# Seven products for six of eight chunk pairs in the up projection, the first conv tap on ScalarE, and five raw buffers

## The chip, the core and the metric

The kernel runs on one core of a Trainium2 chip. The core has engines that run side by side, each with its own queue in program order: TensorE (PE in the profile, with its weight loads as PEld), VectorE (DVE), ScalarE (ACT), GpSimd (POOL) and SyncE (SP), which here only issues DMAs. They wait for each other by semaphores. The metric is the device time of one execution in microseconds; a run of the kernel is compared by the median of its times.

## The reference

One layer of a hybrid encoder for 256 prompt frames and 8 streams of 16 frames, together 384 frames ("tokens", three blocks of 128), all in float32. The part that matters here is the feed-forward half:

```python
h2 = rmsnorm(x, norm_ffn_g)
up = h2 @ w_up                       # (384, 2048) @ (2048, 11264)
g_half, u_half = up[..., :D_FF], up[..., D_FF:]      # D_FF = 5632
ext_f = concat([ffn_buf, g_half])
gc = causal_dwconv(ext_f, ffn_dw_w, ffn_dw_b)        # 3 taps per column
x = x + (silu(gc) * u_half) @ w_down                 # (384, 5632) @ (5632, 2048)
```

The two last gate rows per stream (`new_ffn`) are outputs too.

## The kernel before

Every float32 matrix product is done with operands split in two: `hi` is the value rounded to the type that TensorE multiplies fast, `lo` is the rest, and each product takes three matmuls (hi by hi, hi by lo, lo by hi; function `three`, lines 1352 to 1354). A weight tile of two 128-row chunks and 512 columns (512 KB) is loaded by SP into a raw buffer, copied to `hi` by ScalarE (`CAST hi<-raw`) and reduced to `lo` by VectorE (`TENSOR_TENSOR lo<-raw,hi`).

The feed-forward part works in eleven groups of 512 gate columns and the 512 up columns that belong to them. The order is: up 0, then for g = 1 to 10 up g and down g-1, then down 10. Groups 0 and 10 do the up projection plainly: 16 chunks, 2 column halves, 3 token blocks, 3 matmuls, 288 in all. Groups 1 to 9 save matmuls: for a pair of feature chunks (2k, 2k+1), with token blocks 0 and 1 and the gate and up columns, the four-by-two product is done in the Strassen-Winograd way, with seven products where eight stand in the plain form; token block 2 is done plainly. The sums of activation blocks that it needs are made once (`sums`), the sums of weight blocks must be made for each pair from the raw tiles.

`WINO_STEPS` lists the steps of such a group. A step consumes one split weight tile:

- `s`: a raw gate tile, 12 matmuls. `b`: second chunks of two pairs' up columns, 12 matmuls.
- `c`: two chunks in the plain form, by way of a `differ` block: one gate tile and one up tile, 18 matmuls each.
- `t`: the transformed weights of a pair. Two raw tiles (up and gate) are loaded, VectorE makes three subtractions of 128x512 for the first step (`U`, 9 matmuls) and one more for the second (`G`, 6 matmuls); function `combine`.

Before, pairs 0 to 3 (chunks 0 to 7) have the seven-product form and chunks 8 to 15 the plain one. A group's down projection is 8 steps of 18 matmuls.

The order of the work is written out by a small planner in Python that runs when the kernel is built. `step(mults, products)` emits, for the step j that TensorE now does: the `hi` copy of step j+2, the copies out of the accumulators that the last step finished (`fins`), the matmuls, `combine` for step j+3, the `lo` of step j+2, and the next loads (`load_ahead`, as long as a raw buffer is free). There are three `hi` and three `lo` buffers, so the `hi` of step j+2 can start only when TensorE has done step j-1. Into what time is left it fills the work of `finish_up`, which turns the gate and up rows to feature order (three transposes on VectorE into `tb`, then 16 small DMAs `uT<-tb`, half from SP and half from POOL), copies the gate to `extf` (ACT), fills in the two rows ahead of each block of 16 (`halo`), does three conv taps in four column parts each (`tap`), the SiLU, the product with the up half, and the split of the result into `act`. What it fills in is decided by estimated costs (`now`, `todo`, `work`). Each engine executes what it was given in just this order.

Raw buffers: three own tiles (`raw`) and three in a tile that has become free (`raws`), used in turn. The load for step n can go out when the step that used its buffer, n-6, has its `lo`.

Of the kernel before, what the change touches and what calls it, by code (L numbers as in the profile page):

```python
# [15 lines left out]
P = 128  # L16
DM = 2048
NT = 384
# [23 lines left out]
def hybrid_step(  # L42
# [98 lines left out]
    def stream_tile():  # L141
        made[2] += bool(banks)
        i = made[2] % 6 if banks else 0
        if i < 3:
            return rp.tile([P, 2, 512], F32, tag="raw", bufs=3, name="raw")
        return f(res["raws"][:]).rearrange("p x m t -> p (x m t)")[:, 1024 * (i - 3):1024 * (i - 2)].rearrange(
            "p (k n) -> p k n", k=2)
# [45 lines left out]
    for g in range(1, 11):  # L193
# [3 lines left out]
    WINO_STEPS = [("s", 0), ("s", 1), ("b", 0), ("s", 2), ("s", 3), ("b", 2), ("c", 8), ("t", 0), ("c", 10), ("t", 1),  # L197
                  ("c", 12), ("t", 2), ("c", 14), ("t", 3)]
# [9 lines left out]
    for what, g in FFN_PLAN:  # L208
        if what == "up" and g in WINO:
# [4 lines left out]

            for kind, i in WINO_STEPS:
                if kind == "s":
                    plan.append(two(2 * i, gc))
                elif kind == "b":
                    plan.append([w_up[0, 2 * i * P:(2 * i + 4) * P, uc]
                                 .rearrange("(j c p) n -> p c j n", c=2, p=P)[:, 1]])  # L220
                elif kind == "c":
                    plan.append(two(i, gc))
                    plan.append(two(i, uc))
# [346 lines left out]
    cw = cp.tile([P, CW * 8], F32, name="cw")  # L570
# [446 lines left out]
    def norm_panel(n):  # L1017
# [7 lines left out]
        if n < KP // 2:  # L1025
# [16 lines left out]
    KP = 4  # L1042
# [7 lines left out]

    def diff_of(n, part):
        d = res["dHL"][:, part].rearrange("p m x -> p (m x)")
        o = 4 * P * (n - KP // 2)
        return d[:, o:o + 4 * P].rearrange("p (m i) -> p m i", m=4)

    def split_diff(n):
        nc.scalar.copy(diff_of(n, 0), diff_rows(n))
        tt(diff_of(n, 1), diff_rows(n), f(diff_of(n, 0)), op=ALU.subtract)
# [9 lines left out]
    def wo_done(n):  # L1068
        def done():
            if n == 1:  # L1070
                old_states()
            if n == 3:
                res["dHL"] = gp.tile([P, 2, 4, NT], F32R, tag="G3", name="dHL")
                for i in range(KP // 2, 3):
                    split_diff(i)
            norm_panel(n)
            if n == 3:
                split_diff(3)
                second_norm()
        return done  # L1080
# [18 lines left out]
    res["raws"] = gp.tile([P, 2, 4, NT], F32R, tag="G2", name="raws")  # L1099
# [16 lines left out]
    MM, HI, LO, SUM, RAWS, MOVES, SLACK = 0.227, 1.05, 1.22, 0.7, 6, 7.5, 0.8  # L1116
# [10 lines left out]
    todo = {"DVE": [], "ACT": []}  # L1127
# [75 lines left out]
    fins = []  # L1203

    def step(mults, products):

        t = now["PE"]
        for e in ("ACT", "DVE"):
            now[e] = max(now[e], t)
# [28 lines left out]
        for e in ("ACT", "DVE", "ACT"):  # L1238
            work(e, end + SLACK)
        now["PE"] = end  # L1240

    class Turn:
# [10 lines left out]
        def move(self):  # L1253
            self.ft = p_f.tile([P, 4, 4, NTT, 32], F32, tag="uT", bufs=1, name="uT")
            for a in range(4):
                for q in range(4):
                    (G if q % 2 else S).dma_start(self.ft[32 * q:32 * q + 32, a].rearrange("p m t j -> p (m t j)"),
                                                  self.tb[32 * a:32 * a + 32, q].rearrange("p m t j -> p (m t j)"))
# [4 lines left out]
        def moves(self):  # L1263
            return [("POOL", MOVES, 2.5, self.move)]
# [18 lines left out]
    def finish_up(g, tiles, ready, both=True):  # L1283
# [6 lines left out]
        def halo():  # L1290
            G.tensor_copy(extf[:, :, 1:16, 0:2], extf[:, :, 0:15, 16:18])
            G.tensor_copy(extf[:, :, 16:24, 0:2], sfT[:, 4 * g:4 * g + 4, :].rearrange("p m (b r) -> p m b r", r=2))

        def tap(w, m):
# [4 lines left out]
            if w == 0:  # L1299
                V.tensor_scalar(o, v, wc, col[:, R_FDB + c:R_FDB + c + 1], op0=ALU.mult, op1=ALU.add)  # L1300
# [16 lines left out]
        conv = [("POOL", 1.4, 0.3, halo)]  # L1317
        conv += [("DVE", 0.5 if w == 0 else 0.64, 0.1, lambda w=w, m=m: tap(w, m)) for w in range(3) for m in range(4)]
# [7 lines left out]
        move_u = joined(2, ut.moves() + last)  # L1326
        gate = gt.blocks() + gt.moves() + [[copies + [[move_u, conv + last]], ut.blocks() + move_u if both else [], out]]
# [28 lines left out]
    def wino(g):  # L1356
# [10 lines left out]
        for kind, i in WINO_STEPS:  # L1367
# [4 lines left out]
            elif kind == "c":  # L1372
                steps.append([[(tok(k, 0), 2), (tok(k, 1), 4), (tok(k, 2), "g")] for k in (i, i + 1)])
                steps.append([[(differ(k), 3), (tok(k, 1), 5), (tok(k, 2), "u")] for k in (i, i + 1)])
# [4 lines left out]
        cut = sum(2 if kind in "ct" else 1 for kind, _ in WINO_STEPS[:first_t])  # L1379
# [99 lines left out]
    chain(20.0, [("DVE", 1.7, 0.0, turn_states)])  # L1479
# [54 lines left out]
```

## Time and profile before

| what | us |
|---|---|
| median of 3 runs (1971.16 to 1972.33) | 1972.22 |
| the profiled execution: its own time | 1972.51 |
| its span in the trace | 1970.8 |
| TensorE busy | 1960.6 |
| VectorE busy | 1389.2 |
| ScalarE busy | 808.2 |
| GpSimd busy | 160.0 |
| the feed-forward part begins (first row of L1352) | 913.4 |
| group 5: up projection, down projection of group 4 | 62.6, 32.7 |

Rows of the profile give the line of the kernel, the engine, the operation, what is written and from what, the shape, and busy time, mean, and the idle time of the engine ahead of it with what ended it. Instructions that go through the in-order helper all stand under line 1110, so they are told apart by their tiles. In the table of stretches the columns are: the stretch, its length, busy time (and count) of PE, PEld, DVE, ACT and POOL, the granted clock of TensorE, the busy share of the DMA engines, and GB/s.

### The profile page before, as it was taken

To read this page: it belongs to the slowest core of one execution; us is meant where nothing else is said; L and a number is where in the kernel's file an instruction comes from. 1 tells how busy PE (TensorE), PEld (TensorE's weight loads), DVE (VectorE), ACT (ScalarE), POOL (GpSimd) and SP (SyncE) were. 2 spreads that over 40 slices of the span, in tenths; PEclk is the share of its full clock that TensorE was granted. 3 is DMA by queue.
4 is the path that set the end of the run, shared out by engine and by line. 5 is a ranking of instruction groups with operands and counts; after the bars stand their busy time and mean duration, and the time that the engine had idled before them with its cause. 6 is when DMAs were issued, how large, how long until landed. Compare 5 with 4: busy or idle time off the path is not lost.

```text
span 1970.8 us, 25327 instructions
## 1 busy us (share of the span) xinstructions
PE 1960.6 (99%) x9264; PEld 1655.2 (84%) x9264; DVE 1389.2 (70%) x1918; ACT 808.2 (41%) x1119; POOL 160.0 (8%) x320
## 2 busy tenths in 40 slices
PE   9999999999999999999999999999999999999999
PEld 9888999888888888888888888888888888888887
DVE  4456879788764578677577777777777777777655
ACT  5535454433333523444443434343434344343332
POOL 1000011100000000000102020202020101101120
PEclk9999999999999999999999999999999999999999
DMA  6564777444443333644566565656565655555452
GB/s 184 151 182 119 214 168 152 139 146 129 134 131 126 122 128 120 198 139 150 157 195 190 178 191 172 193 171 193 171 193 174 189 181 183 181 184 188 145 164 103
DMA packets 235408, 321.68 MB, mean 163 GB/s; under 512 B 60219, under 2 KB 105974, under 8 KB 235276
## 3 DMA queue, kind: packets, MB, share of 16 engines
q1 hardware_dynamic: 228083, 310.06, 51.3%
q0 software_dynamic: 7168, 10.00, 2.0%
q8 instruction: 72, 1.18, 0.3%
q14 instruction: 53, 0.43, 0.1%
q10 hardware_dynamic: 32, 0.01, 0.0%
HBM read 295.29 MB, written 7.86 MB: 154 GB/s over the span
## 4 chain that ended last, share of the span: by engine, by line
PE 97%; DVE 2%; DMA 1%; SPq 0%; issue 0%; ACT 0%; DVEq 0%; ACTq 0%
PE bank L1354 18%; PE bank L1352 18%; PE bank L1353 18%; PE acc L311 8%; PE acc L313 8%; PE acc L312 8%; PE misc L312 4%; PE misc L313 4%; PE misc L311 4%; PE acc L306 2%; PE acc L307 2%; PE acc L308 2%; DVE lo L168 0%; DVE mixT L330 0%; DMA raw<-in_w_in_dram 0%; DMA bs<-c_dr 0%
## 5 line engine op out<-in xcount | busy, mean ns | idle before, releaser
L168 DVE TENSOR_TENSOR lo<-raw,hi 128x1024 fp32r<-128x1024 f32 (+2 forms) x219 | 259.3, 1184 | 199.9 <-ACT hi L167 198.1
L167 ACT CAST hi<-raw 128x1024 fp32r<-128x1024 f32 (+2 forms) x219 | 221.7, 1012 | 398.3 <-PE misc L313 308.5
L1110 ACT CAST hi<-raws 128x1024 fp32r<-128x1024 f32 x157 | 165.6, 1055 | 333.0 <-PE bank L1354 315.0
L1352 PE MATMUL bank<-hi,xg 128*128 128x512 f32 x768 | 298.8, 389 | 0.0
L1353 PE MATMUL bank<-lo,xg 128*128 128x512 f32 x768 | 298.8, 389 | 0.0
L1354 PE MATMUL bank<-hi,xg 128*128 128x512 f32 x768 | 298.8, 389 | 0.0
L1110 DVE TENSOR_TENSOR lo<-raw,hi 128x1024 fp32r<-128x1024 f32 x159 | 194.5, 1223 | 131.9 <-ACT hi L1110 131.9
L1110 DVE TENSOR_TENSOR lo<-raws,hi 128x1024 fp32r<-128x1024 f32 x157 | 191.9, 1222 | 135.5 <-ACT hi L1110 135.5
L1110 ACT CAST hi<-raw 128x1024 fp32r<-128x1024 f32 x159 | 166.8, 1049 | 278.1 <-PE bank L1354 200.2
L1352 PE MATMUL bank<-hi,act 128*128 128x512 f32 x528 | 205.4, 389 | 0.0
L1353 PE MATMUL bank<-lo,act 128*128 128x512 f32 x528 | 205.4, 389 | 0.0
L1354 PE MATMUL bank<-hi,act 128*128 128x512 f32 x528 | 205.4, 389 | 0.0
L311 PE MATMUL acc<-hi,hT 128*128 128x512 f32 (+1 forms) x512 | 193.0, 377 | 0.4 <-ACT hT L371 0.4
L313 PE MATMUL acc<-hi,hT 128*128 128x512 f32 (+1 forms) x512 | 190.5, 372 | 0.2
L312 PE MATMUL acc<-lo,hT 128*128 128x512 f32 (+1 forms) x512 | 190.5, 372 | 0.1
L1353 PEld LDWEIGHTS bank<-lo,xg 128*128 128x128 f32 x768 | 144.1, 188 | 30.0
L1354 PEld LDWEIGHTS bank<-hi,xg 128*128 128x128 f32 x768 | 144.1, 188 | 30.0
L1352 PEld LDWEIGHTS bank<-hi,xg 128*128 128x128 f32 x768 | 144.1, 188 | 29.9
L828 DVE SCALAR_TENSOR_TENSOR ut<-ext,cw,ut 128x384 f32<-128x384 f32 x240 | 152.0, 633 | 6.0
L1110 POOL DMA_DIRECT2D uT<-tb x176 | 87.0, 502 | 845.4 <-DMA raw<-in_w_up_dram 722.1
L1353 PEld LDWEIGHTS bank<-lo,act 128*128 128x128 f32 x528 | 99.1, 188 | 20.7
L1352 PEld LDWEIGHTS bank<-hi,act 128*128 128x128 f32 x528 | 99.1, 188 | 20.6
(348 smaller groups left out, 3387.9 us busy)
## 6 DMA issues: line engine op xcount, KB each, us to landing
raws<-in_w_up_dram SPq DMA_DIRECT2D x123, 512.0 KB
raw<-in_w_up_dram SPq DMA_DIRECT2D x107, 512.0 KB
raw<-in_w_in_dram SPq DMA_DIRECT2D x96, 512.0 KB
raw<-in_w_down_dram SPq DMA_DIRECT2D x54, 512.0 KB
raws<-in_w_down_dram SPq DMA_DIRECT2D x34, 512.0 KB
raw<-in_w_in_dram SPq DMA_DIRECT2D x64, 256.0 KB
raw<-in_w_out_dram SPq DMA_DIRECT2D x32, 512.0 KB
uT<-tb SPq DMA_DIRECT2D x176, 48.0 KB
```

What stands on the lines that cost most here:

```text
L167: queued(nc.scalar.copy(hi[:, k, :o], raw[:, k, :o]), first)
L168: queued(tt(lo[:, k, :o], raw[:, k, :o], f(hi[:, k, :o]), op=ALU.subtract), first)
L306: mm(o, hi[:, kk, s], ah, start=st, stop=False)
L307: mm(o, hi[:, kk, s], al, start=False, stop=False)
L311: mm(o, ah[:, s], hi[:, kk, :n], start=st, stop=False)
L312: mm(o, ah[:, s], lo[:, kk, :n], start=False, stop=False)
L313: mm(o, al[:, s], hi[:, kk, :n], start=False, stop=sp)
L828: stt(o, v, wc, o, op0=ALU.mult, op1=ALU.add)
L1110: d = op(*args, **kw)
L1352: mm(o, ah, h[:, kk, :], start=start, stop=False, **kw)
L1353: mm(o, ah, l[:, kk, :], start=False, stop=False, **kw)
L1354: mm(o, al, h[:, kk, :], start=False, stop=stop, **kw)
```

## The change

Groups 1 to 9 do pairs 0 to 5 in the seven-product form; chunks 12 to 15 stay plain. A plain step pair is taken apart (`cg`, `cu`), and the transforms `t` stand between its halves. The activation sums of the third pair of pairs are split into `hi` and `lo` after the feed-forward part has begun (`late`), and the differences are split for chunks 12 to 15 alone. The first conv tap (with the bias) and the two halo copies go from VectorE and GpSimd to ScalarE. The raw buffers are five, three and two. The turning DMAs go into the plan in four parts of four (two from SP, two from POOL) instead of one of sixteen, on a planned time of SP. Two functions that the change adds (`foresee`, `spare`) fill a list that nothing reads. The conv weights `cw` go to another pool.

```diff
     def stream_tile():
         made[2] += bool(banks)
-        i = made[2] % 6 if banks else 0
+        i = made[2] % 5 if banks else 0
...
-    WINO_STEPS = [("s", 0), ("s", 1), ("b", 0), ("s", 2), ("s", 3), ("b", 2), ("c", 8), ("t", 0), ("c", 10), ("t", 1),
-                  ("c", 12), ("t", 2), ("c", 14), ("t", 3)]
+    WINO_STEPS = [("s", 0), ("s", 1), ("b", 0), ("s", 2), ("s", 3), ("b", 2), ("s", 4), ("s", 5), ("b", 4), ("t", 0), ("cg", 12),
+                  ("t", 1), ("cu", 12), ("t", 2), ("cg", 14), ("t", 3), ("cu", 14), ("t", 4), ("t", 5)]
...
-    cw = cp.tile([P, CW * 8], F32, name="cw")
+    cw = p_cv.tile([P, CW * 8], F32, name="cw")
...
-            sums = res["sums"][n]
-            nc.scalar.copy(sums[:, 0], tm)
-            tt(sums[:, 1], tm, f(sums[:, 0]), op=ALU.subtract)
+            if n < 2:
+                sums = res["sums"][n]
+                nc.scalar.copy(sums[:, 0], tm)
+                tt(sums[:, 1], tm, f(sums[:, 0]), op=ALU.subtract)
+            else:
+                res["late"] = tm
...
-    KP = 4
+    KP = 6
...
-    MM, HI, LO, SUM, RAWS, MOVES, SLACK = 0.227, 1.05, 1.22, 0.7, 6, 7.5, 0.8
+    MM, HI, LO, SUM, RAWS, SLACK = 0.227, 1.05, 1.22, 0.7, 5, 0.8
...
-    todo = {"DVE": [], "ACT": []}
+    todo = {"DVE": [], "ACT": [], "SP": []}
...
     def load(dst, srcs):
+        now["SP"] += 0.5
...
-        for e in ("ACT", "DVE", "ACT"):
+        for e in ("SP", "ACT", "DVE", "ACT", "SP"):
             work(e, end + SLACK)
...
-            return [("POOL", MOVES, 2.5, self.move)]
+            return [("SP", 1.4, 0.0 if a < 3 else 6.0, lambda a=a: self.move(a)) for a in range(4)]
...
         def halo():
-            G.tensor_copy(extf[:, :, 1:16, 0:2], extf[:, :, 0:15, 16:18])
-            G.tensor_copy(extf[:, :, 16:24, 0:2], sfT[:, 4 * g:4 * g + 4, :].rearrange("p m (b r) -> p m b r", r=2))
+            A.copy(extf[:, :, 1:16, 0:2], extf[:, :, 0:15, 16:18])
+            A.copy(extf[:, :, 16:24, 0:2], sfT[:, 4 * g:4 * g + 4, :].rearrange("p m (b r) -> p m b r", r=2))
...
             if w == 0:
-                V.tensor_scalar(o, v, wc, col[:, R_FDB + c:R_FDB + c + 1], op0=ALU.mult, op1=ALU.add)
+                A.activation(o, v, AF.Identity, scale=wc, bias=col[:, R_FDB + c:R_FDB + c + 1])
...
-    chain(20.0, [("DVE", 1.7, 0.0, turn_states)])
+    chain(17.0, [("ACT", 1.3, 0.2, lambda: A.copy(res["sums"][2][:, 0], res["late"])),
+                ("DVE", 1.5, 0.2, lambda: V.tensor_tensor(res["sums"][2][:, 1], res["late"], f(res["sums"][2][:, 0]),
+                                                          op=ALU.subtract)),
+                ("ACT", 0.6, 0.2, lambda: A.copy(diff_of(3, 0), diff_rows(3))),
+                ("DVE", 0.65, 0.2, lambda: V.tensor_tensor(diff_of(3, 1), diff_rows(3), f(diff_of(3, 0)), op=ALU.subtract)),
+                ("DVE", 1.7, 0.0, turn_states)])
```

What it moves shows best in the order of the instructions. First VectorE in the up projection of group 7, from the `lo` of the second step of the first `t` on, as it was. A `raw` or `raws` row of 128x512 is a subtraction of `combine` (x3: those of a `U` step), `act` rows are the last of group 6's `finish_up`:

```order
L1110 TENSOR_TENSOR lo<-raw,hi 128x1024
L1110 TENSOR_TENSOR act_12660<-uT,act_12660 128x2x12x32
L1110 TENSOR_TENSOR lo<-raws,hi 128x1024
L1110 TENSOR_TENSOR act_12660<-uT,act_12660 128x2x12x32
L1110 TENSOR_TENSOR lo<-raws,hi 128x1024
L1110 TENSOR_TENSOR raw<-raw 128x512 x3
L1110 TENSOR_TENSOR lo<-raws,hi 128x1024
L1110 TENSOR_TENSOR raw<-raw 128x512
```

Two `lo` of a plain step stood between one transform and the next. The same place now, from the `lo` of both steps of the first `t` on:

```order
L1100 TENSOR_TENSOR lo<-raw,hi 128x1024 x2
L1100 TENSOR_TENSOR act_12727<-uT,act_12727 128x2x12x32
L1100 TENSOR_TENSOR raw<-raws,raw 128x512
L1100 TENSOR_TENSOR raws<-raws 128x512
L1100 TENSOR_TENSOR raws<-raws,raw 128x512
L1100 TENSOR_TENSOR lo<-raws,hi 128x1024
L1100 TENSOR_TENSOR raw<-raw,raws 128x512
L1100 TENSOR_TENSOR lo<-raws,hi 128x1024
L1100 TENSOR_TENSOR lo<-raw,hi 128x1024
L1100 TENSOR_TENSOR act_12727<-uT,act_12727 128x2x12x32
```

The three subtractions of the next transform now stand right behind half of `act`, ahead of the `lo` of the step `cg` 12, and the other half comes three `lo` later.

ScalarE, while group 5 is finished, at the end of a down projection, as it was (`extf` is the padded gate that the conv reads):

```order
L1110 CAST hi<-raw 128x1024
L1110 COPY extf<-uT 128x12x2x16 x3
L1110 CAST hi<-raw 128x1024
L1110 COPY extf<-uT 128x12x2x16
L1110 CAST hi<-raw 128x1024
```

And now:

```order
L1100 CAST hi<-raws 128x1024
L1100 COPY extf<-uT 128x12x2x16 x4
L1100 COPY extf<-extf 128x4x15x2
L1100 COPY extf<-sfT 128x4x8x2
L1100 CAST hi<-raws 128x1024
L1100 ACTIVATE sg<-extf,col,fw 128x384 x4
L1100 CAST hi<-raw 128x1024 x3
```

The halo copies and the four parts of the first tap (`sg<-extf,col,fw`) have come in, between two `hi` copies each.

The queue of SP late in the down projection of group 8, where the gate and then the up rows of group 9 are turned, as it was:

```order
L1110 DMA raw<-in_w_up_dram 128x2x512
L1110 DMA raws<-in_w_up_dram 128x2x512
L1110 DMA uT<-tb 32x384 x8
L1110 DMA raws<-in_w_up_dram 128x2x512 x2
L1110 DMA raw<-in_w_up_dram 128x2x512 x2
L1110 DMA uT<-tb 32x384 x8
```

And the same place now:

```order
L1100 DMA raw<-in_w_up_dram 128x2x512 x2
L1100 DMA uT<-tb 32x384 x4
L1100 DMA raws<-in_w_up_dram 128x2x512
L1100 DMA uT<-tb 32x384 x4
L1100 DMA raws<-in_w_up_dram 128x2x512
L1100 DMA raw<-in_w_up_dram 128x2x512 x2
L1100 DMA uT<-tb 32x384 x4
```

Weight loads that stood in front of or behind a block of eight turning DMAs now stand between its parts.

More of the change, by code (lines that the diff above doesn't have):

```diff
@@ L1316, in finish_up @@
         copies = [("ACT", 0.5, 0.2, lambda a=a: ext_copy(a)) for a in range(4)]
-        conv = [("POOL", 1.4, 0.3, halo)]
-        conv += [("DVE", 0.5 if w == 0 else 0.64, 0.1, lambda w=w, m=m: tap(w, m)) for w in range(3) for m in range(4)]
+        conv = [("ACT", 0.55, 0.2, halo)]
+        conv += [("DVE" if w else "ACT", 0.64 if w else 0.53, 0.1, lambda w=w, m=m: tap(w, m)) for w in range(3) for m in range(4)]
         conv += [("ACT", 0.85, 0.2, lambda h=h: A.activation(tiles.sg[:, 2 * h:2 * h + 2], tiles.sg[:, 2 * h:2 * h + 2],
@@ L1325, in finish_up @@
         last = joined(2, end)
-        move_u = joined(2, ut.moves() + last)
-        gate = gt.blocks() + gt.moves() + [[copies + [[move_u, conv + last]], ut.blocks() + move_u if both else [], out]]
+        move_u = joined(2, ut.moves() + [[out, last]])
+        gate = gt.blocks() + gt.moves() + [[copies + [[move_u, conv + last]], ut.blocks() + move_u if both else []]]
         if both:
```

77 lines of the change are left out of this document (53 added, 24 removed).

## The prediction

> **What bounds the kernel now.** I read the shares of busy time and the chain of waits first, to see which engine sets the end.
>
> ```profile
> span 1970.8 us, 25327 instructions
> ...
> PE 1960.6 (99%) x9264; PEld 1655.2 (84%) x9264; DVE 1389.2 (70%) x1918; ACT 808.2 (41%) x1119; POOL 160.0 (8%) x320
> ...
> PE 97%; DVE 2%; DMA 1%; SPq 0%; issue 0%; ACT 0%; DVEq 0%; ACTq 0%
> ```
>
> TensorE is the chain. Next the waits, and two stretches: group 5's up projection and the down projection behind it.
>
> ```profile
> ACT hi L1110 <- PE bank L1354: 515.2, 234, 3.3
> DVE lo L1110 <- ACT hi L1110: 267.4, 203, 3.1
> ```
>
> ```profile
> 1359.70:1422.30 62.60, 62.60 (x278) 51.82 (x277) 45.45 (x54) 28.09 (x30) 0.00 (x0) 1.00 0.55 175
> 1422.30:1455.00 32.70, 32.70 (x146) 27.09 (x145) 25.50 (x33) 10.90 (x15) 10.49 (x21) 1.00 0.64 195
> ```
>
> ScalarE waits for TensorE to give a `hi` buffer free, VectorE for ScalarE, and TensorE for nobody: it is full in both stretches at a granted clock of 1.00. Fewer matmuls are then worth their whole time, as long as nobody becomes late.
>
> **What the matmuls give.** First rows of two operand groups, one up 0 and one up 1 apart:
>
> ```profile
> L1352 PE MATMUL bank<-hi,xg x768: 389/389/389, 913.4 to 1900.1; 128*128 128x512 f32 x192
> L1352 PE MATMUL bank<-hi,act x528: 389/389/389, 1041.3 to 1965.4; 128*128 128x512 f32 x176
> ```
>
> Between 913.4 and 1041.3 lie 288 + 276 = 564 matmuls: 0.2268 us each. A group had 4x12 + 2x12 + 4x36 + 4x15 = 276 and has 6x12 + 3x12 + 2x36 + 6x15 = 270; nine groups lose 54. That is 54 x 0.2268 = 12.25 us.
>
> **What VectorE and ScalarE get.** The stretch with the first transform in group 5, on VectorE, with ScalarE's `hi` ahead of it:
>
> ```profile
> 1384.22 1.05 ACT L1110 CAST hi<-raw 128x1024 fp32r<-128x1024 f32 x1 [1.55 <-issue]
> ```
>
> ```profile
> 1385.30 1.23 DVE L1110 TENSOR_TENSOR lo<-raw,hi 128x1024 fp32r<-128x1024 f32 x1 [0.77 <-ACT hi L1110]
> 1386.44 0.69 DVE L1110 TENSOR_TENSOR raws<-raw,raws 128x512 f32<-128x512 f32 x1
> 1387.16 0.69 DVE L1110 TENSOR_TENSOR raw<-raw 128x512 f32<-128x512 f32 x1
> 1387.89 0.69 DVE L1110 TENSOR_TENSOR raw<-raw,raws 128x512 f32<-128x512 f32 x1
> 1388.50 1.22 DVE L1110 TENSOR_TENSOR lo<-raw,hi 128x1024 fp32r<-128x1024 f32 x1
> 1389.63 0.68 DVE L1110 TENSOR_TENSOR raws<-raws,raw 128x512 f32<-128x512 f32 x1
> 1390.23 1.22 DVE L1110 TENSOR_TENSOR lo<-raw,hi 128x1024 fp32r<-128x1024 f32 x1
> ```
>
> From start to start a `lo` takes 1.13, three subtractions 2.06, one 0.60; a `lo` starts 1.08 behind its `hi` and its result stands 1.23 later. A transformed pair costs VectorE 2.06 + 1.13 + 0.60 + 1.13 = 4.92 us against 15 x 0.2268 = 3.40 on TensorE. Grouped rows of group 5's up and the down behind it price the rest:
>
> ```profile
> L1110 DVE TENSOR_TENSOR act<-uT,act 128x768 fp32r<-128x768 f32 x2 | 1.9, 951 | 0.0
> L1110 DVE TENSOR_SCALAR sg<-extf,fw,col 128x384 f32<-128x384 f32 x4 | 1.7, 474 | 0.0
> ```
>
> Per group VectorE gets eight subtractions (2 x 2.66 = 5.3) and three `lo` (25 tiles instead of 22, 3.4) and loses the first tap (1.7): 7.0 more. In the stretch from the first transform to the last, six pairs, four plain `lo`, two halves of `act` (0.87 apart, for 1.9) and one accumulator row (0.66) ask 29.5 + 4.5 + 1.7 + 0.7 = 36.4 us, and TensorE does 162 matmuls in 36.7. VectorE is as full as TensorE there, so the order decides; I follow it instruction by instruction.
>
> Time 0 is where TensorE starts the first `t` (t0); its steps then start at 2.04 (t0's second), 3.40 (cg 12), 7.48 (t1), 9.52, 10.88 (cu 12), 14.96 (t2). The `hi` of t0's second step starts with the step before, at -2.72 (12 matmuls); its `lo` at -1.6, VectorE free at -0.5. Half of `act` to 0.4. Three subtractions for t1 to 2.45. `lo` of cg 12 from 2.45, its result at 3.68. TensorE needs it with that step's second matmul, 3.40 + 0.23 = 3.63: late by 0.05, and 0.05 more for the semaphore. Then the single subtraction to 4.2, `lo` of t1 to 5.3, of its second step to 6.6 (its `hi` waits for that subtraction), `act` to 7.4, t2's subtractions to 9.5, `lo` of cu 12 done at 10.75, wanted at 11.1: 0.35 spare. Followed on in the same way, cg 14 has 1.0 and cu 14 0.6 spare, the four `t` steps at the end 0.9 to 1.2, and the down steps more, as VectorE's light steps come then. So one step per group is late.
>
> What a late `lo` costs, the trace of before shows once, at the very start:
>
> ```profile
> 13.63 0.88 DVE L168 TENSOR_TENSOR lo<-raw,hi 128x688 fp32r<-128x688 f32 x1 [3.91 <-ACT hi L167]
> 14.56 0.19 PEld L312 LDWEIGHTS acc<-lo,hT 128*128 128x128 f32 x1 [0.24 <-DVE lo L168]
> ```
>
> The result stands at 14.51, and the matmul's weight load starts at 14.56: the wait sits ahead of the weight load, which is then no longer hidden. By that row a late `lo` costs the 0.10 above and up to 0.19; with the weights already there it would cost 0.10. I take 0.20, nearer the row: 9 x 0.20 = 1.8 us, between 0 (VectorE 0.1 earlier) and 9 x 0.29 = 2.6.
>
> On the page "TensorE: Matmul & The Clock Gate", section "Step-by-step: what each phase is for", the Trainium skill says that TensorE pulls weight loads ahead of matmuls in flight. By that rule these weights (activations, long there) would be loaded in time, each late `lo` would cost 0.10, and the sum would be 0.9 us lower. The row at 14.56 speaks against it where a wait stands in between.
>
> ScalarE gets three `hi` (1.05), four taps, two halo copies per group, 6 us or so:
>
> ```profile
> L1110 ACT COPY extf<-uT 128x384 f32<-128x384 f32 x4 | 1.9, 515 | 0.0
> 1446.73 1.06 ACT L1110 CAST hi<-raw 128x1024 fp32r<-128x1024 f32 x1 [2.61 <-PE bank L1354]
> 1448.38 0.82 POOL L1110 COPY extf<-extf 128x120 f32<-128x120 f32 x1
> ```
>
> No row has a tap on ScalarE; from 0.43 (four copies in 1.9, less the overlap) to 0.68 (a full accumulator row), I take 0.5. The work falls into down steps of 4.08 us, where ScalarE idles 2.6 to 3 ahead of a `hi`: nothing on the path, 3 us per group if it were not covered. Halo on ScalarE between 0.2 and 0.82: the same cover.
>
> **Five buffers and SP.** A load for step n can go out when `lo` n-5 stands.
>
> ```profile
> 1398.12 0.37 SPq L1110 DMA_DIRECT2D raws<-in_w_up_dram  x1
> ```
>
> ```profile
> 1399.00:1400.00 1.00, 1.00 (x6) 0.84 (x5) 0.96 (x2) 0.00 (x0) 0.00 (x0) 1.00 0.72 154
> 1400.00:1401.00 1.00, 1.00 (x7) 0.81 (x6) 1.00 (x2) 0.69 (x1) 0.00 (x0) 1.00 0.95 365
> 1401.00:1402.00 1.00, 1.00 (x6) 0.84 (x5) 1.00 (x3) 0.36 (x1) 0.00 (x0) 1.00 0.02 6
> ```
>
> One load, issued at 1398.12, has its bytes in 1399.0 to 1401.0: landed 3.0 us after issue, of which 2.0 move bytes. The tightest is t2's second tile: out when `lo` of cg 12 stands, 3.7, wanted at 7.4; 3.7 us for 3.0, or up to 5.0 if another load's 2.0 stands in front. I take 0: the load in front of it, t2's first tile, goes out at -0.4, with the `lo` of t0's second step, and has landed by 2.6. In the 2.72 us steps ahead a load has five steps less 2.4, some 11 us.
>
> The turning DMAs stand among loads on SP in the down steps and the first `s` steps:
>
> ```profile
> SPq L1110 <- DVE tb L1110: 11.2, 11, 1.2
> ```
>
> SP waits 1.2 at most for a transpose, with loads queued behind; these have 8 us to spare (11 less 3.0), so 0. With that cover gone, 1.2 per group, 11 us. POOL loses the halo copies and waits as before. The work that moves at the end of the output projection (five half-size additions for one subtraction, at most 2.8 us) falls in front of `lo` rows that TensorE wants 3 us later: 0. `late` is first read in group 1, over 60 us behind the start of the feed-forward part.
>
> At the end, the second half of group 10's `act` stands behind the last `lo` of down 9: 2.35 into a step of 4.08, and 0.87 more; 0.8 us to spare, so 0, and 0.9 if it slips by a `lo`.
>
> **Sum.** 1972.51 (profiled execution, 0.29 over the median) - 12.25 + 1.8 = 1962.1; against the median 1961.8. I say 1962.0.
>
> **Rivals.**
> - VectorE is the bound. Where 36.4 us of work meet 36.7, each wait of VectorE for a `hi` (0.77 in the row at 1385.30) may come out on TensorE. For: the count above. Against: VectorE starts the stretch two steps ahead and has 0.35 or more in hand at every step but one. Up to 0.8 us per group, 7 in all: 1969.
> - Slower: starved of weights. If the loads of a transform go through one behind the other, each lands at about 3.0 + 2.0 = 5.0, and VectorE, in order, stands 1.3 us at three of six pairs, with every `lo` behind it late: 3.9 less 0.35 us per group, 32 us, 1992. For: five buffers, and the share of 0.95 that one load alone reaches. Against: loads are issued at each `lo`, mostly over 1.1 us apart. It turns slower from 1.8 us per group on (12.25 + 3.9, over 9).
> - SP is late: a load behind a waiting turn comes 1.2 us late on the path: 11 us, 1973, no change. Against: the 8 us in hand.
> - That the matmuls don't go away is excluded: the order has 8820 rows of TensorE for 8874.
>
> **Chances.** Less than 0.2% (4 us) can't be told from no change. The forecast, 1959.6 to 1965: 0.70. VectorE as bound, to 1969: 0.16. SP, 1968.3 to 1976.2: 0.05. Starved: 0.09. So faster 0.86, same 0.05, slower 0.09. The range runs from 1959.6 (no stall, less 0.4 for runs) to 1969.0.
>
> **What would show it.** TensorE: 54 matmuls fewer, nine short waits for a `lo`, at cg 12, none over 0.5 us. VectorE's busy time up by 50 to 65 us, its waits for ScalarE down. ScalarE's waits for raw tiles and VectorE's waits for DMA near zero; if these are tens of microseconds, the loads were the mistake. If TensorE waits at the last `t` steps, VectorE was.

## The result and the profile after

The changed kernel takes 1965.05 us (median of nine runs, 1963.65 to 1967.4) beside 1971.96 us for the kernel before on the same chip (nine runs, 1970.28 to 1972.39). The ratio is 0.9968 with a 95% interval of 0.9958 to 0.9978: 6.9 us less. The forecast was 10 us less, 1962.0, so 3 us of it are missing. 1965.05 lies inside the range given, 1959.6 to 1969.0, and 0.05 over the part of it (1959.6 to 1965) that stood for the forecast itself.

The page of the changed kernel (its profiled execution took 1964.78 us), its shares of busy time and its chain of waits:

```profile
span 1963.1 us, 25493 instructions
...
PE 1951.5 (99%) x9210; PEld 1644.6 (84%) x9210; DVE 1448.3 (74%) x1977; ACT 869.7 (44%) x1212; POOL 150.4 (8%) x298
...
PE 94%; DVE 4%; issue 1%; DMA 1%; ACT 1%; SPq 0%; ACTq 0%; DVEq 0%
```

There are 54 matmuls fewer (9210 for 9264), VectorE is busy 59 us longer and ScalarE 61 us, and VectorE, which had 2% of the chain, has 4%. The waits show what is new (engine, what it was about to do, what ended the wait: us in total, times, longest):

```profile
PEld bank L1377 <- DVE lo L1100: 7.1, 14, 0.7
PE bank L1377 <- DVE lo L1100: 1.9, 10, 0.3
DVE raw L1100 <- DMA raw<-in_w_up_dram: 6.1, 8, 1.6
DVE raws L1100 <- DMA raws<-in_w_up_dram: 3.4, 6, 0.9
```

TensorE waits for a `lo` at fourteen places, and VectorE, which had waited for no weight load worth a row, waits for one at fourteen as well. (The line numbers are those of the changed kernel: 1376 to 1378 are the three matmuls of a product, 1100 is the in-order helper.) The same two stretches as before, group 5's up projection and the down projection behind it:

```profile
1355.67:1417.45 61.78, 61.62 (x272) 50.53 (x270) 52.11 (x61) 31.10 (x33) 0.00 (x0) 1.00 0.67 202
1417.45:1450.09 32.64, 32.64 (x146) 27.04 (x144) 25.36 (x34) 13.88 (x20) 9.48 (x19) 1.00 0.68 201
```

The up projection is 0.82 us shorter where six matmuls fewer are 1.36: here 0.54 us per group are lost. VectorE's work in it went from 45.45 to 52.11, the 6.7 us more being close to the 7.0 that were counted. The down projection behind it is as long as it was.

Where most of those 0.54 us are, the timeline tells. VectorE from the second `lo` of `t0` on, in group 5:

```profile
1378.76 1.23 DVE L1100 TENSOR_TENSOR lo<-raw,hi 128x1024 fp32r<-128x1024 f32 x1 [1.14 <-ACT hi L1100]
1379.90 0.95 DVE L1100 TENSOR_TENSOR act<-uT,act 128x768 fp32r<-128x768 f32 x1
1380.77 2.14 DVE L1100 TENSOR_TENSOR raws<-raws 128x512 f32<-128x512 f32 x3
1382.83 1.22 DVE L1100 TENSOR_TENSOR lo<-raw,hi 128x1024 fp32r<-128x1024 f32 x1
```

And TensorE's matmuls at the start of `cg` 12:

```profile
1383.33 0.39 PE L1378 MATMUL bank<-hi,xg 128*128 128x512 f32 x1
1383.56 0.39 PE L1376 MATMUL bank<-hi,xg 128*128 128x512 f32 x1
1384.10 0.50 PE L1377 MATMUL bank<-lo,xg 128*128 128x512 f32 x1 [0.16 <-DVE lo L1100]
1384.43 0.40 PE L1378 MATMUL bank<-hi,xg 128*128 128x512 f32 x1
```

The weight loads of the last two:

```profile
1384.10 0.19 PEld L1377 LDWEIGHTS bank<-lo,xg 128*128 128x128 f32 x1 [0.58 <-DVE lo L1100]
1384.21 0.19 PEld L1378 LDWEIGHTS bank<-hi,xg 128*128 128x128 f32 x1
```

Half of `act`, three subtractions, and then the `lo` of `cg` 12, whose result stands at 1382.83 + 1.22 = 1384.05. TensorE began the step at 1383.56 and wanted this `lo` 0.227 later, at 1383.79. Its matmul starts at 1384.10, 0.31 late, and the next one follows after 0.33 instead of 0.227. The weight load of the waiting matmul, which elsewhere starts with the matmul before it, starts at 1384.10 too, and the next weight load 0.11 behind it. Together that is 0.42 us.

The starts of all matmuls in the feed-forward part, one after the other, show how often this happens. Everything that lies more than 0.03 us over the 0.2268 of a matmul, summed by place:

```
place                                  times   lost us
lo of cg 12, groups 1 to 9                 9      4.0   (each 0.42 to 0.49, the two gaps together)
lo of cu 12, groups 2 and 6                2      0.8   (0.59 and 0.23)
two single gaps, groups 5 and 8            2      0.15
first to last matmul of the part: 1052.41 before, 1045.60 after: 6.81 less
54 x 0.2268 = 12.25 less, 4.96 lost in these gaps, 0.5 in gaps too small for the list
```

So the matmuls gave what they were said to give, and 5.4 us came back. The theory at this point: the place of one `lo` on VectorE costs 4 us, and loads that land late a fifth of that. The rivals: five buffers are the real cause; VectorE is as full as TensorE and would only be late elsewhere; or the rest of the change (ScalarE's new work, the turning DMAs) costs something.

### The profile page after: what moved, and what is told of

Its sections match the earlier page's. It is cut to its first block, busy times and chain, and to the rows that moved or that the text cites. A ratio compares the mean times of both kernels' runs of the same rounds, so it can differ in the third digit from the quotient of the medians.

```text
span 1963.1 us, 25493 instructions
## 1 busy us (share of the span) xinstructions
PE 1951.5 (99%) x9210; PEld 1644.6 (84%) x9210; DVE 1448.3 (74%) x1977; ACT 869.7 (44%) x1212; POOL 150.4 (8%) x298
## 4 chain that ended last, share of the span: by engine, by line
PE 94%; DVE 4%; issue 1%; DMA 1%; ACT 1%; SPq 0%; ACTq 0%; DVEq 0%
PE bank L1377 17%; PE bank L1378 17%; PE bank L1376 16%; PE acc L314 8%; PE acc L312 8%; PE acc L313 8%; PE misc L314 4%; PE misc L313 4%; PE misc L312 4%; PE acc L307 2%; PE acc L309 2%; PE acc L308 2%; DVE lo L1100 1%; DVE raw L1100 0%; ACT hi L1100 0%
## 5 line engine op out<-in xcount | busy, mean ns | idle before, releaser
L1100 ACT CAST hi<-raw 128x1024 fp32r<-128x1024 f32 x207 | 217.4, 1050 | 327.2 <-PE bank L1378 273.3
L1100 DVE TENSOR_TENSOR lo<-raw,hi 128x1024 fp32r<-128x1024 f32 x207 | 252.4, 1221 | 114.7 <-ACT hi L1100 111.8
L1377 PE MATMUL bank<-lo,xg 128*128 128x512 f32 x696 | 271.9, 391 | 1.5 <-DVE lo L1100 1.5
L1376 PE MATMUL bank<-hi,xg 128*128 128x512 f32 x696 | 270.9, 389 | 0.0
L1378 PE MATMUL bank<-hi,xg 128*128 128x512 f32 x696 | 270.8, 389 | 0.0
L1100 ACT CAST hi<-raws 128x1024 fp32r<-128x1024 f32 x136 | 143.4, 1054 | 215.4 <-PE bank L1378 182.2
L1100 DVE TENSOR_TENSOR lo<-raws,hi 128x1024 fp32r<-128x1024 f32 x136 | 166.0, 1221 | 80.2 <-ACT hi L1100 77.8
L1377 PEld LDWEIGHTS bank<-lo,xg 128*128 128x128 f32 x696 | 130.6, 188 | 32.5 <-DVE lo L1100 5.6
L1376 PEld LDWEIGHTS bank<-hi,xg 128*128 128x128 f32 x696 | 130.7, 188 | 27.4
L1378 PEld LDWEIGHTS bank<-hi,xg 128*128 128x128 f32 x696 | 130.7, 188 | 26.7
L1376 PEld LDWEIGHTS bank<-hi,act 128*128 128x128 f32 x528 | 99.1, 188 | 20.6
L1378 PEld LDWEIGHTS bank<-hi,act 128*128 128x128 f32 x528 | 99.1, 188 | 20.5
```

Of the source, the lines that this page charges most:

```text
L1100: d = op(*args, **kw)
L1376: mm(o, ah, h[:, kk, :], start=start, stop=False, **kw)
L1377: mm(o, ah, l[:, kk, :], start=False, stop=False, **kw)
L1378: mm(o, al, h[:, kk, :], start=False, stop=stop, **kw)
```

## The experiments

All are the changed kernel with one edit, timed beside the kernel before. "Lost" is the sum of the list above for that kernel's trace.

**1. The activation behind the `lo` of `cg` 12.** The planner may not issue the activation's subtractions in the two steps ahead of that `lo`:

```diff
-                if max(ready, now[eng]) + cost <= until:
+                if max(ready, now[eng]) + cost <= until and not (hold[0] and cost == 0.971):
...
             room[0] += 1
+        if hold[0] == 2:
+            hold[0] = 0
...
-                 ("DVE", 0.97, 0.2, lambda h=h: V.tensor_tensor(part(1, h), ft(h), f(part(0, h)), op=ALU.subtract))]
+                 ("DVE", 0.971, 0.2, lambda h=h: V.tensor_tensor(part(1, h), ft(h), f(part(0, h)), op=ALU.subtract))]
...
+            hold[0] = 1 if j == cut - 1 else 2 if j == cut else 0
             step(3 * sum(len(x) for x in halves), products)
```

> The first half of the activation of the group before is subtracted behind the lo of step cg 12 instead of ahead of it, and the second half one place later as well; no operation is added or taken away. Theory (the order on VectorE makes that lo late, 0.43 us in each of nine groups): the lo stands 0.87 us earlier, the nine waits of TensorE at cg 12 go to zero, the two longer ones at cu 12 (groups 2 and 6, a load that comes late there) stay, and the time falls by 3.9 us against the changed kernel, to 1961.1 (1960 to 1962). Rival (loads into five buffers are what is late): nothing changes, 1965. Second rival (VectorE is as full as TensorE in that stretch, so a delay only moves): the 0.43 us come back at cu 12 or cg 14, 1964 to 1966.

Measured: 1963.39 us (1963.17 to 1964.26), ratio to before 0.9961 (0.9947 to 0.9974). Lost: 3.10 for 4.96. The place is right, the prize smaller than expected: the median lies between the 1960 to 1962 of the theory and the 1964 to 1966 of the second rival. In six groups the wait at `cg` 12 is gone. VectorE in group 5, where the same three subtractions and the same `lo` now follow at once on the `lo` of `t0`:

```profile
1378.27 1.23 DVE L1100 TENSOR_TENSOR lo<-raw,hi 128x1024 fp32r<-128x1024 f32 x1 [1.14 <-ACT hi L1100]
1379.41 2.14 DVE L1100 TENSOR_TENSOR raws<-raws 128x512 f32<-128x512 f32 x3
1381.47 1.22 DVE L1100 TENSOR_TENSOR lo<-raw,hi 128x1024 fp32r<-128x1024 f32 x1
```

The `lo` stands at 1382.69, 0.6 ahead of its matmul at 1383.29. In group 1 the wait stays (0.42), because there it is half of the activation's multiplication that stands in front. And waits come where VectorE stands for a load: 0.74 in group 7 and 0.33 in group 3 at `cg` 12, 0.59 in group 5 at `cg` 14, 0.45 in group 8 at `cu` 14 (three smaller ones sum to 0.57). Group 7:

```profile
1566.62 1.23 DVE L1100 TENSOR_TENSOR lo<-raw,hi 128x1024 fp32r<-128x1024 f32 x1 [1.14 <-ACT hi L1100]
1568.93 0.69 DVE L1100 TENSOR_TENSOR raw<-raws,raw 128x512 f32<-128x512 f32 x1 [1.09 <-DMA raw<-in_w_up_dram]
```

VectorE had come free 1.09 us before the load. That is the first rival, behind the first cause: as long as `act` stood there, it filled the time in which the load was still missing.

**2. The activation's first half twice.**

```diff
-                 ("DVE", 0.97, 0.2, lambda h=h: V.tensor_tensor(part(1, h), ft(h), f(part(0, h)), op=ALU.subtract))]
+                 ("DVE", 0.97, 0.2, lambda h=h: [V.tensor_tensor(part(1, h), ft(h), f(part(0, h)), op=ALU.subtract)
+                                                 for _ in range(2 - h)])]
```

> The first half of the activation is subtracted twice, one instruction behind the other, ahead of the lo of cg 12. Theory: the lo, late already, comes 0.87 us later and all of it is lost, 9 x 0.87 = 7.8 us, up to 0.9 more at the program's end: 1972.9 to 1973.8. Rival (VectorE has slack there and the wait comes from loads): under 2 us, 1965 to 1967. If VectorE were the bound of the whole stretch and not of one place, each group would lose the same 0.87, but waits would show at cu 12 and cg 14 as well.

Measured: 1973.94 us (1972.0 to 1976.74), ratio 1.0012 (1.0003 to 1.0021), 8.9 more than the changed kernel, 0.1 over the upper end. The second one takes 0.99 us from start to start, since it writes what the first has just written, and the gap at `cg` 12 goes from 0.545 to 1.536 in eight groups (in group 1 the pair stands behind the `lo` and is lost at `cu` 12 and `cg` 14 instead; and at `cu` 12 of group 6, where a load is late, 0.88 is lost for 0.23). Lost: 14.4. The gap behind it stays 0.34. So from the point where the `lo` is late every 0.1 us on VectorE costs 0.1 us, and the 0.11 on the next matmul is a fixed price per wait.

**3. Six raw buffers.**

```diff
-        i = made[2] % 5 if banks else 0
+        i = made[2] % 6 if banks else 0
...
-    MM, HI, LO, SUM, RAWS, SLACK = 0.227, 1.05, 1.22, 0.7, 5, 0.8
+    MM, HI, LO, SUM, RAWS, SLACK = 0.227, 1.05, 1.22, 0.7, 6, 0.8
```

> Six raw buffers instead of five (three and three), everything else as in the changed kernel. Theory: the 9.5 us that VectorE waits for loads go to nearly zero, but only the two waits of TensorE at cu 12 hang on them (0.59 and 0.23 us), so the time falls by 0.5 to 1.0 us, to 1964.1 to 1964.6, and the nine waits at cg 12 stay at 0.43 us. Rival (five buffers cost the missing gain): 3 us less or more, 1962 or below.

Measured: 1964.11 us (1962.87 to 1964.52), ratio 0.9961 (0.9949 to 0.9974): 0.9 less than the changed kernel, as the first theory had it. Its waits:

```profile
PEld bank L1377 <- DVE lo L1100: 5.2, 9, 0.6
```

VectorE waits for no `raw` or `raws` load any more, the two waits at `cu` 12 are gone, and the nine at `cg` 12 stand: lost 3.84.

**4. The change without its centre: four pairs.**

```diff
-    KP = 6
+    KP = 4
...
-    WINO_STEPS = [("s", 0), ("s", 1), ("b", 0), ("s", 2), ("s", 3), ("b", 2), ("s", 4), ("s", 5), ("b", 4), ("t", 0), ("cg", 12),
-                  ("t", 1), ("cu", 12), ("t", 2), ("cg", 14), ("t", 3), ("cu", 14), ("t", 4), ("t", 5)]
+    WINO_STEPS = [("s", 0), ("s", 1), ("b", 0), ("s", 2), ("s", 3), ("b", 2), ("cg", 8), ("cu", 8), ("t", 0),
+                  ("cg", 10), ("cu", 10), ("t", 1), ("cg", 12), ("cu", 12), ("t", 2), ("cg", 14), ("cu", 14), ("t", 3)]
```

(The activation differences of chunks 8 to 15 take the place of the third set of sums in `late`.)

> Only pairs 0 to 3 are done in the seven-product form, as in the kernel before, with all the rest of the change kept (plain steps split in two halves of four steps, first tap and halo on ScalarE, five buffers, turning DMAs in four parts). 54 matmuls come back. Theory: the rest of the change costs nothing, 1972 (1971 to 1973). Rival (the rest of the change costs what is missing from the forecast): 1974.5 to 1976.

Measured: 1971.71 us (1969.85 to 1972.3), ratio 0.9998 (0.999 to 1.0007). The five buffers, the tap and the halo on ScalarE and the parted turning DMAs together cost nothing and bring nothing that can be told (the interval runs from 2.0 us less to 1.4 us more). Lost: 0.23. What is missing from the forecast is tied to the six pairs.

**5. Both cures.** The edits of 1 and 3, and in group 1 the second multiplication is held back too:

```diff
-        end = [[[("DVE", 0.97, 0.2, lambda h=h: mul(h)),
+        end = [[[("DVE", 0.971 if h else 0.97, 0.2, lambda h=h: mul(h)),
```

> Both cures together: the subtractions of the activation behind the lo of cg 12 (in group 1, where its multiplication stands there instead, the second multiplication goes behind that lo too), and six raw buffers. Theory (the place of one lo, and then loads into five buffers, are all that is missing): every wait of TensorE in the feed-forward part goes, 5.0 us in the trace of the changed kernel, so 1960.0 (1959.5 to 1960.8), 12 us under the kernel before, which is what the 54 matmuls are worth. Rival (VectorE is as full as TensorE there and something else becomes late): waits at cu 12 or cg 14, 1961.5 to 1963.5.

Measured: 1960.43 us (1959.6 to 1961.23), ratio 0.9943 (0.9931 to 0.9956): the fastest of all, 4.6 under the changed kernel and 11.3 under the kernel before in the same comparison. Its page's shares, and below them its only wait of this kind:

```profile
PE 1948.4 (99%) x9210; PEld 1645.3 (84%) x9210; DVE 1448.2 (74%) x1977; ACT 869.8 (44%) x1212; POOL 149.8 (8%) x298
```

```profile
PEld bank L1380 <- DVE lo L1100: 0.6, 1, 0.6
```

VectorE does the same 1448 us of work as in the changed kernel and TensorE loses 0.43 us in all, in group 1, where the first multiplication has slipped into the place of the second:

```profile
1002.16 1.23 DVE L1100 TENSOR_TENSOR lo<-raw,hi 128x1024 fp32r<-128x1024 f32 x1 [1.49 <-ACT hi L1100]
1003.31 0.95 DVE L1100 TENSOR_TENSOR uT<-uT,sg 128x768 f32<-128x768 f32 x1
```

So VectorE is not the bound of the stretch. The two cures are worth more together than alone: with `act` in its old place the sixth buffer brought 0.9 us, with `act` out of the way 3.0 (1963.39 to 1960.43; the edit for group 1 has no part in it, its wait is 0.43 in both).

**6. Four raw buffers.** As 3, with 4 in both places.

> Four raw buffers instead of five, everything else as in the changed kernel. Theory (five buffers are just enough, the load for a transform lands up to 1 us late at some places): with four each load goes out one lo later, 1.1 to 2 us, so VectorE waits 0.5 to 1.5 us at most of the transforms and TensorE behind it: 1975 to 1992. Rival (loads have several us to spare): under 1968.

Measured: 2065.41 us (2062.94 to 2071.24), ratio 1.048 (1.0465 to 1.0496): 100 us more. The theory's direction is right and its size far off; why each wait is so long, no run takes apart. The waits:

```profile
DVE raw L1100 <- DMA raw<-in_w_up_dram: 97.1, 40, 4.2
DVE raws L1100 <- DMA raws<-in_w_up_dram: 28.0, 13, 3.5
...
PEld bank L1377 <- DVE lo L1100: 93.5, 53, 4.1
```

53 waits of VectorE, 2.4 us each on average, where 0.5 to 1.5 were expected. One of them, in group 8: SP issues a load, another one 1.34 us behind it, and VectorE's next subtraction, which waits for the first of them, starts 4.89 us after its issue.

```profile
1742.03 0.37 SPq L1100 DMA_DIRECT2D raw<-in_w_up_dram  x1
```

VectorE's timeline at that place, which stands idle for 2.71 us in between:

```profile
1743.26 0.95 DVE L1100 TENSOR_TENSOR act<-uT,act 128x768 fp32r<-128x768 f32 x1
1746.92 2.15 DVE L1100 TENSOR_TENSOR raw<-raw 128x512 f32<-128x512 f32 x3 [2.71 <-DMA raw<-in_w_up_dram]
```

And TensorE's, whose matmul comes 3.89 us behind the one before it (that one started at 1746.37):

```profile
1750.26 0.50 PE L1377 MATMUL bank<-lo,xg 128*128 128x512 f32 x1 [3.50 <-DVE lo L1100]
...
1752.03 0.63 PE L1377 MATMUL bank<-lo,xg 128*128 128x512 f32 x1
1752.46 0.63 PE L1378 MATMUL bank<-hi,xg 128*128 128x512 f32 x1
```

The gaps between matmuls in the feed-forward part sum to 87 us. Another 19 are in matmuls like the last two rows, and the section on the hardware comes back to them.

**7. The first tap on VectorE again, the halo on GpSimd.**

```diff
-            A.copy(extf[:, :, 1:16, 0:2], extf[:, :, 0:15, 16:18])
+            G.tensor_copy(extf[:, :, 1:16, 0:2], extf[:, :, 0:15, 16:18])
...
-                A.activation(o, v, AF.Identity, scale=wc, bias=col[:, R_FDB + c:R_FDB + c + 1])
+                V.tensor_scalar(o, v, wc, col[:, R_FDB + c:R_FDB + c + 1], op0=ALU.mult, op1=ALU.add)
...
```

(The planner's entries for them go back as well.)

> The first tap goes back to VectorE and the halo copies to GpSimd; all else as in the changed kernel. If VectorE's and ScalarE's idle time in the down steps covers either place, 1965 (1964.3 to 1965.8). If the 1.7 us per group that VectorE gets back come out on TensorE, up to 17 us more; if only the later end of the convolution matters, since the activation then stands at another place, 1 to 3 us more.

Measured: 1966.25 us (1964.93 to 1967.28), ratio 0.9973 (0.9962 to 0.9984). The median is 1.2 over the changed kernel's 1965.05 and 0.8 over that of its second measurement (below), with ranges that overlap; the traces lose 5.27 and 4.96 us. That is no difference that can be told: the tap is covered on either engine, though VectorE works 17 us longer with it.

**8. The turning DMAs in one batch.** `move` issues all sixteen at once, as before the change, with the planned entry `("POOL", 7.5, 2.5, self.move)`.

> The sixteen turning DMAs go out as one batch again, as in the kernel before, instead of four parts; all else as in the changed kernel. If the place of these DMAs on SP does not bear on the time, 1965 within 0.8. If loads queue behind a batch that waits for its transposes (1.2 us), up to 11 us more. If the split itself cost something in the changed kernel, 1 to 3 us less.

Measured: 1966.73 us (1964.4 to 1968.29), ratio 0.9975 (0.9966 to 0.9984): 1.7 over the changed kernel, with intervals that overlap. Lost: 7.34 for 4.96. VectorE waits longer for loads than in the changed kernel (13.2 us in 15 waits, for 9.5 in 14):

```profile
DVE raw L1100 <- DMA raw<-in_w_up_dram: 7.8, 9, 2.3
DVE raws L1100 <- DMA raws<-in_w_up_dram: 5.4, 6, 1.2
```

**9. Six buffers and one batch.** The edits of 3 and 8.

> Six raw buffers and the sixteen turning DMAs in one batch; the rest as in the changed kernel. If a batch costs time only because the weight loads behind it come late into five buffers, then with six it costs nothing: 1964.1 (1963.4 to 1964.9), the nine waits of TensorE at cg 12 as before and no others. If a batch costs something else (the turned rows come later, and the activation with them), the 1.7 us between one batch and four parts stay: 1965.5 to 1966.5.

Measured: 1964.1 us (1963.32 to 1964.34), ratio 0.996 (0.9948 to 0.9973), the same as six buffers alone (1964.11); lost 3.92 for 3.84. So what the batch costs in the traces, 2.0 to 2.4 us, comes through loads that are late into five buffers; the medians alone could not show it, as their intervals are 2 us and more wide.

**10. The changed kernel once more**, beside 9.

> The changed kernel once more, beside the run above on one chip, to tell whether the 1.2 us of the tap and the 1.7 us of the batch are differences at all: 1965.05 is what its runs gave before (1963.65 to 1967.4). A median of 1965.0 to 1965.5 leaves both as small losses; 1966 or more makes them no difference.

Measured: 1965.46 us (1964.8 to 1967.19), ratio 0.9968 (0.9956 to 0.998). Lost: 5.35, and the nine waits at `cg` 12 at the same places. The waits for late loads differ between these two traces of one kernel: at `cu` 12 group 2 loses 0.12 for 0.59 and group 6 0.70 for 0.23. Against this run the batch is 1.3 us slower and the tap 0.8, by the bounds set ahead two small losses: the first has its cause in the trace and in run 9, the second has none.

## Why the prediction came out as it did

**The matmuls: right.** 54 x 0.2268 = 12.25 was the whole gain, and run 5 shows it on the path almost to the last: from first to last matmul of the feed-forward part 1040.63 us for 1052.41, 11.78 less, with 0.43 still lost.

**One step per group late, at `cg` 12: right in place, number and kind; its size was the term that failed.** The step as put there was "late by 0.05, and 0.05 more for the semaphore", and with the weight load 0.20 us in each of nine groups, 1.8 in all, between 0 and 2.6. Measured are 0.42 to 0.49 each, 4.0 in all, over the upper bound. Taken apart on the rows of group 5: the semaphore is 0.05 (1384.05 to 1384.10), as said; the weight load costs 0.11, close to the 0.10 taken; but the `lo` is 0.26 late and not 0.05. The ledger was off from its first entry, "the `hi` of t0's second step starts with the step before, at -2.72". ScalarE's rows in the changed kernel's timeline:

```profile
1374.96 1.05 ACT L1100 CAST hi<-raw 128x1024 fp32r<-128x1024 f32 x1 [0.94 <-PE bank L1378]
1377.68 1.05 ACT L1100 CAST hi<-raw 128x1024 fp32r<-128x1024 f32 x1 [1.67 <-DVE lo L1100]
```

TensorE's matmuls around the two changes of step:

```profile
1374.49 0.39 PE L1378 MATMUL bank<-hi,xg 128*128 128x512 f32 x1
1374.71 0.39 PE L1376 MATMUL bank<-hi,xg 128*128 128x512 f32 x1
...
1377.21 0.39 PE L1378 MATMUL bank<-hi,xg 128*128 128x512 f32 x1
1377.43 0.39 PE L1376 MATMUL bank<-hi,late 128*128 128x512 f32 x1
```

A step's first matmul starts 0.22 behind the last one of the step before, but that last one holds its `hi` for 0.39. So the `hi` buffer comes free 0.17 after the next step has begun, and ScalarE starts 0.08 behind that: 0.25 after the step's start both times (1374.71 to 1374.96, 1377.43 to 1377.68). The second row names a `lo` of VectorE that ended at 1377.62, 0.02 behind the matmul; that the distance is the same where the row names TensorE speaks for the matmul. So do the other groups: of the 239 waits for TensorE ahead of a `hi` in the changed kernel, 238 end 0.20 to 0.25 us behind the first matmul of a step, and in the kernel before 232 of 234. (The end of a matmul is modelled in the profile; these distances are between starts.) Everything behind it on VectorE stood 0.20 to 0.25 later than the ledger had it, and by run 2 all of that is lost. The row of before that would have told it was in the prediction: a matmul's 389 ns beside the pitch of 0.2268.

**The weight load of a late `lo`: not hidden, as the row at 14.56 said.** On the page "TensorE: Matmul & The Clock Gate", section "Step-by-step: what each phase is for", the Trainium skill says that weight loads are pulled ahead of matmuls in flight. Here the weight load starts at 1384.10, together with its matmul, and the one behind it 0.11 later. The prediction took such a row to speak against the rule, but it does not: in both traces the wait for `lo` stands in the weight load itself (none of the 4590 matmuls of the changed kernel's feed-forward part carries one), though its weights are activations that are long there. Whether 0.11 us per wait would be saved if the matmul waited instead, no run shows.

**VectorE's and ScalarE's work: right.** VectorE is busy 59.1 us more (50 to 65 were said) and ScalarE 61.5, and VectorE's waits for ScalarE ahead of a `lo` fell, as said, from 267.4 us to 189.7; runs 4 and 7 put the cost of the tap and the halo at nothing that can be told from zero.

**Five buffers at 0: wrong by a little.** The text took 0, since the load in front "goes out at -0.4" and "has landed by 2.6", and expected VectorE's waits for DMA "near zero"; they are 9.5 us, and 0.8 of it came out on TensorE at `cu` 12, where I had 0.35 us in hand; one of the two waits there is 0.59, over the 0.5 that was to be the most. In group 2 SP's rows have the late load first in a pair:

```profile
1100.46 2.11 SPq L1100 DMA_DIRECT2D raws<-in_w_up_dram  x2
```

VectorE's wait for the first of them, in its timeline:

```profile
1105.25 0.69 DVE L1100 TENSOR_TENSOR raws<-raw,raws 128x512 f32<-128x512 f32 x1 [0.87 <-DMA raws<-in_w_up_dram]
```

4.8 us from issue to use, inside the 3.0 to 5.0 that the text gave, and I took the near end. Two readings made it too short. A load counts up a semaphore as it lands, and by these counts in the trace the load of before, issued at 1398.12, landed at 1401.51: 3.4 us after its issue, where 3.0 was the time to its last bytes. And the load in front had not landed by 2.6: in group 2 it went out at 1096.41 with another still under way (that one landed at 1098.66) and landed at 1101.33, 4.8 us after the start of `t0`. The price is 0.9 us by run 3, and 3.0 with `act` out of the way (runs 1 and 5). The rival in which the weights starve did not come true with five buffers, but it was one buffer away: with four, a case that its 3.9 us per group did not price, it is 100 us, 11 per group.

**SP at 0: right for the change as made.** With one batch it would have been 1.3 to 1.7 us by the medians, through the buffers (runs 8 and 9).

**The ends at 0: in keeping with the traces.** From the start of the last matmul to the end of the span are 5.0 us in both kernels. The feed-forward part starts at 912.5 for 913.4 before, and among the traces of all the kernels here, most of them with the same early part, it starts between 911.7 and 913.8, so that nothing can be read from 0.9.

The sum again, on the profiled executions: 1962.1 was forecast and 1964.78 came. 2.2 of the difference is the size of the `cg` 12 term (4.0 for 1.8), 1.0 the waits at `cu` 12 and the two single gaps, 0.5 small gaps, and -1.0 the earlier start, which lies within the scatter above. That the time lies in the range is luck in part: by the bounds of its own terms the sum could reach 1972.51 - 12.25 + 2.6 = 1962.9, and the room up to 1969.0 was left for VectorE as the bound, which run 5 rules out.

## What to carry to other kernels

A ledger that follows one engine instruction by instruction finds the place where two full engines meet, but it is worth its tenths only if a buffer is taken as free when the last matmul that reads it ends, and not when the next one starts (here 0.20 to 0.25 us). Where an engine is within a few tenths of another, the cheapest cure is the order: an operation that nobody wants for some 35 us (the activation, which the down projection reads) does not belong ahead of one that is wanted at once. And two causes can hide behind one another: the sixth buffer looked like 0.9 us until the order was mended, and then it was 3.0, so a cure that brings little is to be tried again once the next one is in.

## What the runs showed of the hardware that was not expected

**What a late operand costs TensorE.** In the rows above: the lateness itself, 0.05 us until the matmul starts, and 0.11 on the next matmul. With the lateness 0.99 larger (run 2) the last figure is the same (gaps of 0.335 to 0.341 behind every wait at `cg` 12, in both). In the trace it is the weight load that waits; that the 0.11 is this load, no longer hidden, is my reading of the rows and was not tested.

**TensorE at half clock behind waits.** With four buffers the matmuls come 0.427 us apart instead of 0.227 for a while after some of the waits, and the granted clock says why. Three stretches of run 6 (behind the length: busy time and count of PE, PEld, DVE, ACT and POOL, granted clock, DMA share, GB/s): the wait, the slow matmuls, and the ones after them.

```profile
1746.40:1750.20 3.80, 0.36 (x2) 0.00 (x0) 3.21 (x5) 0.97 (x1) 0.00 (x0) 1.00 0.15 59
...
1751.60:1754.60 3.00, 3.00 (x9) 2.32 (x8) 2.44 (x3) 0.42 (x1) 0.00 (x0) 0.50 0.76 221
1754.90:1757.90 3.00, 3.00 (x14) 2.44 (x13) 0.77 (x2) 1.05 (x1) 0.00 (x0) 1.00 0.66 248
```

There are twelve such stretches with 96 matmuls at some 0.427, each 0.20 too long: 19 us. The Trainium skill says on the page "TensorE: Matmul & The Clock Gate", section "Part 1: The HAM clock gate (the "warmup" mystery)", that the clock falls to half after an idle window of about 3.4 us and returns after a busy one. The trace agrees in part: the seven longest gaps between two matmuls, 2.84 to 4.04 us, were all followed by a slow stretch, most of which last 3.0 us; but so were five gaps of 2.18 to 2.80 us, and fifteen between 1.98 and 2.78 were not. In the changed kernel the longest gap is 0.71 us, and its clock stays at full speed.

Which gaps did it shows in the clock's own records in the trace. In the feed-forward part of run 6 the granted clock changes only at the marks of a raster of 3.41 us, and each half-clock stretch fills one interval of it, two of them two. All eleven full-clock intervals in which TensorE was busy for under 1.4 us were followed by one at half clock, and of the eleven with 1.58 to 2.01 us a single one was; so TensorE need not be idle for the whole of it. A gap of 2.42 us at 1256.51, which lies inside one interval, cost the clock; and one of 2.78 at 1555.00, which two intervals share, did not:

```profile
1256.48:1259.89 3.41, 1.38 (x6) 0.83 (x5) 3.38 (x5) 1.88 (x3) 0.00 (x0) 1.00 0.00 0
1259.89:1263.31 3.42, 3.42 (x10) 2.51 (x9) 3.08 (x3) 1.84 (x2) 0.00 (x0) 0.50 0.70 219
...
1553.44:1556.85 3.41, 1.95 (x9) 1.29 (x7) 2.33 (x4) 0.10 (x1) 0.00 (x0) 1.00 0.25 96
1556.85:1560.26 3.41, 2.48 (x11) 2.04 (x12) 3.02 (x4) 2.00 (x2) 0.00 (x0) 1.00 0.37 100
1560.26:1563.68 3.42, 3.42 (x17) 2.84 (x16) 1.48 (x2) 1.64 (x2) 0.00 (x0) 1.00 0.86 268
```

A wait of TensorE can thus cost more than its length: with four buffers 87 us are the gaps themselves, and 19 come on top.

**A load of 512 KB took 3.4 to 6.2 us from issue to landing, by the median 3.6 with none in front of it and 4.35 with one.** By the semaphore counts in the trace of the changed kernel, as far as they can be told apart, 45 loads of the feed-forward part had none under way in front and took 3.52 to 4.89 us (median 3.62); 238 had one, and took 3.44 to 6.25 (median 4.35). A load behind matters less: eleven had none in front and another issued 1.74 us behind, and ten of these took 3.52 to 3.71. The late load of group 2 (4.77 us, to 1105.23) had 0.87 us of one in front and another 1.74 behind. The bytes came at 207 to 262 GB/s while it was under way from 1102 to 1105, and at 401 in the next microsecond:

```profile
1102.00:1103.00 1.00, 1.00 (x6) 0.84 (x5) 0.88 (x2) 0.26 (x1) 0.00 (x0) 1.00 0.74 262
1103.00:1104.00 1.00, 1.00 (x6) 0.84 (x5) 1.00 (x2) 0.00 (x0) 0.00 (x0) 1.00 0.85 219
1104.00:1105.00 1.00, 1.00 (x6) 0.81 (x5) 0.39 (x1) 0.28 (x1) 0.00 (x0) 1.00 0.72 207
1105.00:1106.00 1.00, 1.00 (x6) 0.84 (x5) 0.71 (x2) 0.78 (x1) 0.00 (x0) 1.00 1.04 401
```

Why the bytes came more slowly there, no run here tells.
